# Rotation, modulation columns, masks and staged rows moved in a one-core trunk step

## The chip, the core and the metric

The kernel runs on one core of a Trainium2 chip. The metric is the device time of one launch in microseconds. TensorE is called PE (PEld are its weight loads), VectorE DVE, ScalarE ACT, GpSimd POOL, and SyncE SP; SP and POOL issue the DMAs.

## The reference

One layer of a hybrid trunk over 640 tokens (512 latent, 128 context) of width 1024: a gated feed-forward half-step, a token mixer, a second half-step, each behind a norm whose scale and shift (adaLN) come from a conditioning vector. Of the mixer, cut to what matters here:

```python
dq = rmsnorm(dq.reshape(B, T, DA_HEADS, 2, DA_HEAD_DIM), p['g_qn'][l])
dk = rmsnorm(dk.reshape(B, T, DA_HEADS, 2, DA_HEAD_DIM), p['g_kn'][l])
q_att = rope_2d(dq); keys = jnp.concatenate([rope_2d(dk), k_ctx], axis=1)
...
s = jnp.einsum('bqhcd,bkhcd->bhcqk', qi, kf) * scale
pr = jax.nn.softmax(s, axis=-1)
w = pr[:, :, 0] - lam * pr[:, :, 1]          # two softmaxes to a head
att = rmsnorm(einsum('bhqk,bkhv->bqhv', w, vf), g_sub)
...
# mLSTM, 4 heads, two directions, chunks of 128 tokens, state C carried on
dmat = jnp.exp(log_d - m_t[..., None])       # masked to the causal triangle
s = jnp.einsum('bhtd,bhsd->bhts', qc, kc) * dmat
num = einsum('bhts,bhsv->bhtv', s, vc) + inter * einsum('bhtd,bhdv->bhtv', qc, C)
...
y = sigmoid(gm) * (hm @ w_br_m) + sigmoid(gd) * (att @ w_br_d)
out = y @ w_out
```

The modulation is `silu(c) @ w_ada + b_ada`, 9 vectors of 1024 for each of two conditioning vectors. The outputs are the new tokens, the new keys and values of the context, and its final mLSTM states.

## The kernel before

Everything is float32, computed on PE as three products of split parts (a value is split into a high part and the remainder, and high x high, high x low and low x high are summed). ACT makes the high part of a weight (`wH`), DVE the low part (`wL`), from a raw row that SP loads.

The order of work on PE is the program's order (`mm` and `tr` keep it). The order of instructions on ACT, DVE, and the DMA queues is chosen by the scheduler when the kernel is built; each engine then works its list in order. `tc.issue_after(x)` puts the instructions of a block behind `x` on `x`'s engine.

*Attention, 8 heads* (profile from about 520 to 1075 us). Queries, keys and values are projected for pairs of heads. `qk_norm_rope` norms the projected rows and rotates them: the swapped copy `sw` on ACT, then on DVE `sw` times `B`, the rows times `A`, their sum, and the context tokens' gain. `Head.queries` and `Head.keys` turn the rows on PE into `ps_qkT`, ACT and DVE split them into `qT`, `kH` and `kL`, and POOL copies the halves of the keys to the other partitions. For each of five blocks of 128 queries: `scores` (PE into `sc`, then the softmax on DVE and ACT: `mx`, `nm`, two exponentials, `rc`, `r`, and `p`, kept as `at_p[qi]`), `turn` of the block before (PE into `ps_wT`), and `values` of it (PE into `ps_o`, DVE into `ao`, kept as `at_out`). Block 4 holds context tokens only and is short. After the last block comes the turn of the next head's queries and keys; if the next head is of a new pair, its keys must have been made (`made`).

Between these, `Fill` puts product units of other projections from a queue, so that PE has work while a softmax runs: `slot` runs at least one unit, and more where the pacing (`pace`, time per slot) says so. The units' results are evacuated into two staged rows (`stage`) and stored by SP: `o_evac` (DVE and ACT), `gate_evac` and `v_evac` (ACT). Two units stand ahead of head 0's first scores. The rows of the mLSTM gates are worked out in steps (`gate_rows`) beside head 0.

*Modulation columns.* `Columns.tile` loads a block of the turned modulation weights (512 KB, `raw_a`) and reduces it on DVE against the two conditioning vectors, two instructions of 128x1024 (`junk`). In attention eight tiles are placed in head 2 through one buffer, two after the values of each block from block 0 to block 3:

```python
            if qi > 0:
                H.values(qi - 1)
                if hd == 2:
                    columns.tile(H.at_out)
                    columns.tile(H.at_p[qi])
```

*mLSTM, 4 heads* (about 1075 to 1230 us). `Memory.load` brings values and the row of stabilisers, spread over the partitions, into `P`, and DVE adds the masks behind the last preparation of the head before. `prep` turns the keys, forms `ps_st`, takes the exponentials of `P` on ACT (`exps`) and multiplies on DVE. `cell` runs ten steps (five chunks, two directions): products with `P` and with the state `C`, and the update of `C` on DVE. A list `later` puts parts of the next and the last head behind the cells: preparations of the next head behind cells 3 to 7. `m.gate` loads `so` and takes its logarithm and exponential on ACT. Staged units of the gate projections run between the cells (`gate_evac` with the pool `mp`).

Of the kernel before, what the change touches and what calls it, by code (L numbers as in the profile page):

```python
# [31 lines left out]
def tile_trunk(ctx: ExitStack, tc: tile.TileContext, a: dict):  # L32
# [1137 lines left out]
    def qk_norm_rope(raw, tab, pr):  # L1170
        A, B, g = tab
        if pr:
            sq = ap.tile([128, 5, 256], F32, tag="pk", name="sq", bufs=2)
        else:
            sq = ap.tile([128, 5, 256], F32, tag="qT", name="sq")
        act(sq, raw, AF.Square)
        ss = ap.tile([128, 20], F32, tag="ss", name="ss", bufs=2)
        vec.tensor_reduce(out=ss, in_=sq.rearrange("p t (g d) -> p (t g) d", d=64), axis=AX.X, op=ALU.add)
        rs = rstd_of(ap, ss, 1.0 / 64, [128, 20], "qk")
        r3 = raw.rearrange("p t (g d) -> p (t g) d", d=64)  # L1180
        tt(vec, r3, r3, rs[:, :, None].to_broadcast([128, 20, 64]), ALU.mult)
        sw = ap.tile([128, 4, 256], F32, tag="pk", name="sw", bufs=2)
        act(
            sw.rearrange("p t (b s j) -> p (t b) s j", s=2, j=16),
            raw[:, 0:4, :].rearrange("p t (b s j) -> p (t b) s j", s=2, j=16)[:, :, ::-1, :],
            AF.Copy,
        )
        s4 = sw.rearrange("p t (g d) -> p t g d", d=64)
        q4 = raw[:, 0:4, :].rearrange("p t (g d) -> p t g d", d=64)
        tt(vec, s4, s4, B[:, :, None, :].to_broadcast([128, 4, 4, 64]), ALU.mult)  # L1190
        tt(vec, q4, q4, A[:, :, None, :].to_broadcast([128, 4, 4, 64]), ALU.mult)
        tt(vec, raw[:, 0:4, :], raw[:, 0:4, :], sw, ALU.add)
        p3 = raw[:, 4, :].rearrange("p (g d) -> p g d", d=64)
        tt(vec, p3, p3, g[:, None, :].to_broadcast([128, 4, 64]), ALU.mult)

    q_tok, k_tok, v_tok = {}, {}, {}
    made = set()

    def project_q(pr):
        def make():  # L1200
            q_tok[pr] = t = ap.tile([128, 5, 256], F32, tag="qtok", name="q_tok")

            def evac(p, i):
                act(t[:, i, :], p, AF.Copy)
                if i == 4:
                    qk_norm_rope(t, tabs[0], pr)

            return evac

        return a["w_dq"][pr], make  # L1210

    def project_k(pr):
        def make():
            k_tok[pr] = t = ap.tile([128, 5, 256], F32, tag="ktok", name="k_tok")

            def evac(p, i):
                act(t[:, i, :], p, AF.Copy)
                if i == 4:
                    qk_norm_rope(t, tabs[1], pr)
                    made.add(pr)  # L1220
                    nc.sync.dma_start(out=a["new_k"][:, pr * 256 : (pr + 1) * 256], in_=t[:, 4, :])

            return evac

        return a["w_dk"][pr], make
# [195 lines left out]
    def o_evac(h):  # L1421

        def f(p, mt, hf):
            t = ap.tile([128, HALF], F32, tag="stage", name="stage", bufs=2)
            ts(t, p, -43.0, ALU.max)
            act(t, t, AF.Exp, scale=-1.0)
            nc.sync.dma_start(out=o_dram[:, 2 * h + mt, half(hf)], in_=t)
        return f

    def gate_evac(pool, dst, g):  # L1430
        def f(p, mt, hf):
            t = pool.tile([128, HALF], F32, tag="stage", name="stage", bufs=2)
            act(t, p, AF.Copy)  # L1433
            nc.sync.dma_start(out=dst[:, 2 * g + mt, half(hf)], in_=t)
        return f

# [21 lines left out]
    for _ in range(3):  # L1458
        fill.one()
    heads[0].keys()  # L1460
    for _ in range(2):
        fill.one()
    heads[0].scores(0)

# [21 lines left out]

    def v_evac(h):
        def f(p, i):
            t = ap.tile([128, HALF], F32, tag="stage", name="stage", bufs=2)
            act(t[:, 0:256], p, AF.Copy)  # L1490
            nc.sync.dma_start(out=v_dram[h][:, i, :], in_=t[:, 0:256])
        return f
# [3 lines left out]
    for hd in range(8):  # L1496
        H = heads[hd]
        pr, odd = divmod(hd, 2)
        if not odd:
            fill.granule(a["w_mq"][pr], feat_units(psum, q_evac(pr)))  # L1500
            fill.granule(a["w_mk"][pr], feat_units(psum, k_evac(pr)))
            if pr:
                fill.granule(a["w_mv"][pr], tok_units(psum, v_evac(pr)))
            us = 2 * 13.2 + 13.0
            if hd == 0:
                us += 6 * 3.3
            if pr < 3:
                qk = project_q(pr + 1), project_k(pr + 1)
                fill.granule(qk[0][0], lambda f=qk[0][1]: tok_units(psum, f()), lambda hd=hd: turned > hd)
                fill.granule(qk[1][0], lambda f=qk[1][1]: tok_units(psum, f()), lambda hd=hd: turned > hd)  # L1510
                us += 26.0
            if not pr:
                fill.granule(a["w_mv"][pr], tok_units(psum, v_evac(pr)))
            if pr:
                fill.granule(a["w_mo"][pr], feat_units(psum, o_evac(pr)))
                us += 13.2
            if pr == 3:
                fill.granule(a["w_gd"][0], feat_units(psum, gate_evac(ap, gd_dram, 0)))
                fill.granule(a["w_gm"][1], feat_units(psum, gate_evac(ap, gm_dram, 1)))
                us += 16.0  # L1520
            fill.pace(us, 22)
        for qi in range(5):
            if hd or qi:
                H.scores(qi)
            if hd == 0 and qi < 4:
                with tc.issue_after(H.at_act.ins), tc.issue_after(H.at_p[qi - 1].ins if qi else H.at_vec.ins):
                    next(gates)
            if (hd, qi) == (1, 0):
                place_columns()
            if qi > 0:  # L1530
                H.turn(qi - 1)
            if hd == 1 and qi in (2, 3):
                gate_cols()
            fill.slot()
            if late is not None:
                late()
                late = None
            if hd == 1 and qi in (1, 2):
                gate_load(qi - 1)
            if qi > 0:  # L1540
                H.values(qi - 1)
                if hd == 2:
                    columns.tile(H.at_out)
                    columns.tile(H.at_p[qi])
            if qi < 4:
                fill.slot()
        H.turn(4)
        if hd < 7:
            N = heads[hd + 1]
            while N.pr not in made:  # L1550
                fill.one()
            if odd:
                fill.slot()
                H.values(4)
                src, evac = project_v(pr + 1)
                units = fill.begin(src, tok_units(psum, evac()))
                units[0]()
                N.queries()
                N.keys()
                turned = hd + 1  # L1560
                H.finish_norm()
                for u in units[1:]:
                    u()
            else:
                N.queries()
                N.keys()
                turned = hd + 1
                fill.slot()
                H.values(4)
                H.finish_norm()  # L1570
                fill.slot()
                fill.slot(2)
            late = H.finish
        else:
            fill.slot()
            H.values(4)
            H.finish_norm()
            fill.one()
            fill.one()
            fill.drain()  # L1580
            H.finish()
# [28 lines left out]
    class Memory:  # L1610
# [2 lines left out]
        def __init__(self, h):  # L1613
            self.h, self.cells = h, []

        def load(self, behind=None):
            h = self.h
            queue = nc.sync if h else nc.gpsimd
            self.va = mp.tile([128, 5, 258], F32, tag="va", name="va", bufs=2)
# [4 lines left out]
            for d in range(2):  # L1624
                queue.dma_start(
                    out=self.P[:, :, d, :], in_=nm_dram[32 * d + h].partition_broadcast(128).rearrange("p (c t) -> p c t", c=5)
                )
                with ExitStack() as st:
                    if behind is not None:
                        st.enter_context(tc.issue_after(behind.ins))  # L1630
                    tt(vec, self.P[:, :, d, :], self.P[:, :, d, :], mask[:, d, None, :].to_broadcast([128, 5, 128]), ALU.add)
            self.ktok = mp.tile([128, 5, 256], F32, tag="ktok", name="mktok", bufs=2)
            self.hs = mp.tile([128, 5, 256], F32, tag="hs", name="hs", bufs=2)

        def load_c(self):
            self.C = [mp.tile([128, 2, 258], F32, tag=f"C{d}", name="C", bufs=2) for d in range(2)]
# [7 lines left out]
        def prep(self, i):  # L1644
# [13 lines left out]
            for dt in range(2):  # L1658
                mm(p, k[:, dt, tok], q[:, dt, tok], start=dt == 0, stop=dt == 1)
            if h:  # L1660
                self.exps(i)
            self.at_prep = tt(vec, self.P[:, i], p[:, None, :].to_broadcast([128, 2, 128]), self.P[:, i], ALU.mult)

        def cell(self, i, d, accumulate, inter, update):
# [101 lines left out]
    mem = [Memory(h) for h in range(4)]  # L1766
    mem[0].load()
    mem[0].load_c()
    for i in range(5):
        mem[0].exps(i)  # L1770
    fill.one()
    fill.one()
    for i in range(5):
# [2 lines left out]
    for h in range(4):  # L1776
        m = mem[h]
        later = [[] for _ in range(10)]
        if h < 3:
            mem[h + 1].load(mem[h].at_prep)  # L1780
            for i in range(5):
                later[3 + i].append(lambda i=i: mem[h + 1].prep(i))
        if h > 0:
# [334 lines left out]
```

## Time and profile before

| | |
|---|---|
| median of 3 runs | 1856.08 us (1852.09 to 1860.09) |
| the profiled execution | 1852.26 us |
| its span, mean granted TensorE clock | 1850.4 us, 0.992 |
| PE busy in the span | 1791.7 us (97%) |
| DVE, ACT busy | 1291.0 us (70%), 829.7 us (45%) |

In the rows below, a timeline row has the start and the duration in us, the engine, the line of the kernel, the operation, out<-in with shapes, the count, and in brackets the idle time of the engine before it and what ended it. A row of stages has the stretch and its length, then busy times with counts of PE, PEld, DVE, ACT and POOL, the granted clock, the DMA share and GB/s. A row of waits has total, times and longest. A helper's instructions carry the helper's line: L52 `mm`, L55 `tr`, L39 `tt`, L42 `stt`, L46 and L48 `ts`.

### The profile page before, as it was taken

What the parts mean: (1) busy time and instruction counts of PE and PEld (TensorE: products, weight loads), DVE (VectorE), ACT (ScalarE), POOL (GpSimd) and SP (SyncE); (2) the same over time, 40 slices, a digit from 0 to 9 for tenths busy, and PEclk for the clock granted to TensorE, in tenths of its full rate; (3) what the DMA queues carried; (4) which work ended last, traced back from release to release, by engine and by line L of the source; (5) the groups of instructions that cost most, each with busy time, mean ns of one, the idle gap of its engine ahead of it and who ended that gap; (6) DMA issues with size and microseconds to landing.
All of it is one profiled execution on the core that took longest, in us unless ns stands there. A gap on an engine that the chain in (4) does not pass through costs nothing.

```text
span 1850.4 us, 30491 instructions
## 1 busy us (share of the span) xinstructions
PE 1791.7 (97%) x12498; PEld 1757.3 (95%) x12498; DVE 1291.0 (70%) x2188; ACT 829.7 (45%) x1439; POOL 51.6 (3%) x93
## 2 busy tenths in 40 slices
PE   6999999999999999999999999999999899999989
PEld 4999999999999998999999988899999899999989
DVE  6888885575776657765655557677767778886576
ACT  6654454112644543444443455573336455553232
POOL 0000001110000000000000000000000000000000
PEclk9999999999999999999999999999999999999989
DMA  8344448963324234232232254676652445557952
GB/s 332 130 161 171 155 150 325 328 209 120 119 88 151 73 122 139 74 119 75 83 101 91 97 168 130 208 250 213 211 182 75 154 149 169 189 172 277 342 205 85
DMA packets 127244, 304.98 MB, mean 165 GB/s; under 512 B 9985, under 2 KB 89217, under 8 KB 114433
## 3 DMA queue, kind: packets, MB, share of 16 engines
q1 hardware_dynamic: 116242, 257.09, 40.3%
q0 software_dynamic: 10864, 45.95, 7.2%
q8 instruction: 98, 1.61, 0.3%
q14 instruction: 40, 0.33, 0.1%
HBM read 234.20 MB, written 63.63 MB: 161 GB/s over the span
## 4 chain that ended last, share of the span: by engine, by line
PE 53%; DVE 3%; DMA 2%; ACT 1%; issue 1%; SPq 0%; DVEq 0%; ACTq 0%
PE ps_f L52 23%; PE ps_p L52 19%; PE ps_t L52 5%; PE ps_n L52 2%; PE sc L52 2%; PE ps_o L52 1%; PE ps_u L52 1%; DMA P<-nm_dram 1%; DMA raw_a<-in_w_ada_c 1%; PE ps_wT L55 1%; DVE wL L39 0%; ACT wH L122 0%; DVE k_tok L39 0%; DMA raw<-in_w_gm 0%; PE ps_st L52 0%
## 5 line engine op out<-in xcount | busy, mean ns | idle before, releaser
L52 PE MATMUL ps_f<-S,ww 128*128 128x320 f32 x1992 | 320.5, 311 | 5.5 <-ACT ww L286 3.8
L52 PEld LDWEIGHTS ps_f<-S,ww 128*128 128x128 f32 x1992 | 301.0, 189 | 6.1 <-ACT ww L286 4.1
L52 PE MATMUL ps_p<-hH,wH 128*128 128x320 f32 x864 | 274.1, 317 | 2.8 <-ACT stage L1433 1.6
L52 PE MATMUL ps_p<-hH,wL 128*128 128x320 f32 x864 | 267.6, 310 | 0.0
L52 PE MATMUL ps_p<-hL,wH 128*128 128x320 f32 x864 | 267.5, 310 | 0.0
L52 PE MATMUL ps_f<-hm,ww 128*128 128x320 f32 x1248 | 200.9, 314 | 7.6 <-ACT ww L286 4.1
L52 PEld LDWEIGHTS ps_f<-hm,ww 128*128 128x128 f32 x1248 | 190.3, 192 | 8.7 <-ACT ww L286 4.4
L52 PE MATMUL ps_t<-wH,hH 128*128 128x256 f32 x640 | 184.6, 288 | 4.3 <-ACT stage L1490 2.7
L52 PE MATMUL ps_t<-wH,hL 128*128 128x256 f32 x640 | 181.2, 283 | 1.1 <-DVE hL L39 1.1
L52 PE MATMUL ps_t<-wL,hH 128*128 128x256 f32 x640 | 180.9, 283 | 0.0
L52 PEld LDWEIGHTS ps_p<-hH,wH 128*128 128x128 f32 x864 | 163.1, 189 | 3.9 <-ACT stage L1433 1.9
L39 DVE TENSOR_TENSOR ww<-raw,ww 128x2048 fp32r<-128x2048 f32 (+1 forms) x62 | 138.7, 2237 | 39.9 <-ACT ww L286 26.2
L52 PEld LDWEIGHTS ps_p<-hL,wH 128*128 128x128 f32 x864 | 163.1, 189 | 0.5
L52 PEld LDWEIGHTS ps_p<-hH,wL 128*128 128x128 f32 x864 | 162.8, 188 | 0.0
L52 PE MATMUL ps_f<-hm,wB 128*128 128x320 f32 x1008 | 161.5, 309 | 0.0
L52 PEld LDWEIGHTS ps_f<-hm,wB 128*128 128x128 f32 x1008 | 151.3, 188 | 0.0
L39 DVE TENSOR_TENSOR wL<-raw,wH 128x2048 fp32r<-128x2048 f32 x49 | 112.1, 2288 | 43.7 <-ACT wH L122 43.6
L122 ACT ACTIVATE wH<-raw 128x2048 fp32r<-128x2048 f32 x49 | 93.6, 1911 | 81.7 <-PE ps_p L52 77.0
L52 PEld LDWEIGHTS ps_t<-wH,hH 128*128 128x128 f32 x640 | 122.5, 191 | 5.3 <-ACT stage L1490 2.9
L286 ACT ACTIVATE ww<-raw 128x2048 fp32r<-128x2048 f32 x48 | 91.7, 1911 | 75.0 <-DVE raw L39 63.7
L39 DVE TENSOR_TENSOR raw<-raw 128x1024 f32<-128x1024 f32 x144 | 124.2, 862 | 1.4
L52 PEld LDWEIGHTS ps_t<-wH,hL 128*128 128x128 f32 x640 | 122.5, 191 | 1.5 <-DVE hL L39 1.5
(295 smaller groups left out, 3179.9 us busy)
## 6 DMA issues: line engine op xcount, KB each, us to landing
g_dram<-g SPq DMA_DIRECT2D x44, 640.0 KB, 4.7
raw_a<-in_w_ada_c SPq DMA_DIRECT2D x32, 512.0 KB, 3.9
raw<-in_w1b SPq DMA_DIRECT2D x11, 1024.0 KB, 4.8
raw<-in_w3b SPq DMA_DIRECT2D x11, 1024.0 KB, 6.9
raw<-in_w1a SPq DMA_DIRECT2D x10, 1024.0 KB, 4.8
raw<-in_w3a SPq DMA_DIRECT2D x10, 1024.0 KB, 4.9
hm<-g_dram POOLq DMA_DIRECT2D x8, 1280.0 KB, 10.2
raw_a<-in_w_ada_k SPq DMA_DIRECT2D x8, 1024.0 KB, 11.3
```

The lines of the kernel that those rows point to most:

```text
L39: return eng.tensor_tensor(out=out, in0=in0, in1=in1, op=op)
L52: tc.keep_in_program_order(nc.tensor.matmul(*args, **kw))
L55: tc.keep_in_program_order(nc.tensor.transpose(*args, **kw))
L122: act(h, raw, AF.Copy)
L286: act(t[0], flat, AF.Copy)
```

## The change

The rotation of the keys becomes a generator of two steps. The first, up to the copy `sw`, comes where the whole came; the second is kept in `rotating` and issued, for pairs 1 to 3, behind the last softmax (`at_p[4]`) of the head that runs, and with it the store of the new keys. In attention there are three staged rows; four units instead of two stand ahead of head 0's scores. Of head 2's eight column tiles, one goes ahead of block 0, one behind its softmax, two after the values of blocks 0 and 1, none after block 2, one behind the last softmax and one after the last values. In the mLSTM stage the masks of the next head go behind cell 1, its exponentials behind the current cell's scaling on ACT, and the first staged row's evacuation behind head 0's exponentials.

```diff
             AF.Copy,
         )
+        yield
...
         tt(vec, p3, p3, g[:, None, :].to_broadcast([128, 4, 64]), ALU.mult)
+        yield
+
+    rotating = []
+
+    def rotated(behind=None):
+        while rotating:
+            with ExitStack() as st:
+                if behind is not None:
+                    st.enter_context(tc.issue_after(behind.ins))
+                rotating.pop(0)()
...
                 if i == 4:
-                    qk_norm_rope(t, tabs[1], pr)
-                    made.add(pr)
-                    nc.sync.dma_start(out=a["new_k"][:, pr * 256 : (pr + 1) * 256], in_=t[:, 4, :])
+                    steps = qk_norm_rope(t, tabs[1], pr)
+                    next(steps)
+
+                    def rest():
+                        next(steps)
+                        made.add(pr)
+                        nc.sync.dma_start(out=a["new_k"][:, pr * 256 : (pr + 1) * 256], in_=t[:, 4, :])
+
+                    rotating.append(rest)
+                    if not pr:
+                        rotated()
...
-            t = ap.tile([128, HALF], F32, tag="stage", name="stage", bufs=2)
+            t = ap.tile([128, HALF], F32, tag="stage", name="stage", bufs=3)
...
+    stage_behind = []
     def gate_evac(pool, dst, g):
         def f(p, mt, hf):
-            t = pool.tile([128, HALF], F32, tag="stage", name="stage", bufs=2)
-            act(t, p, AF.Copy)
+            t = pool.tile([128, HALF], F32, tag="stage", name="stage", bufs=2 + (pool is ap))
+            with ExitStack() as st:
+                for ins in stage_behind:
+                    st.enter_context(tc.issue_after(ins.ins))
+                act(t, p, AF.Copy)
+            stage_behind.clear()
...
-    for _ in range(2):
+    for _ in range(4):
         fill.one()
     heads[0].scores(0)
...
             if hd == 0:
-                us += 6 * 3.3
+                us += 4 * 3.3
...
+        if hd == 2:
+            columns.tile(H.at_vec)
         for qi in range(5):
...
             fill.slot()
+            if (hd, qi) == (2, 0):
+                columns.tile(H.at_p[0])
...
                 H.values(qi - 1)
-                if hd == 2:
+                if hd == 2 and qi < 3:
                     columns.tile(H.at_out)
                     columns.tile(H.at_p[qi])
+                if (hd, qi) == (2, 4):
+                    columns.tile(H.at_p[4])
+            if qi == 4:
+                rotated(H.at_p[4])
...
             while N.pr not in made:
                 fill.one()
+                rotated(H.at_p[4])
...
                 H.values(4)
+                if hd == 2:
+                    columns.tile(H.at_out)
                 H.finish_norm()
...
-        def load(self, behind=None):
+        def load(self):
...
+        def masks(self, behind=None):
+            for d in range(2):
                 with ExitStack() as st:
...
             if h:
-                self.exps(i)
+                with tc.issue_after(mem[h - 1].at_act.ins):
+                    self.exps(i)
...
     mem[0].load_c()
+    mem[0].masks()
     for i in range(5):
         mem[0].exps(i)
+    stage_behind.append(mem[0].at_exp)
...
-            mem[h + 1].load(mem[h].at_prep)
+            mem[h + 1].load()
+            later[1].append(lambda: mem[h + 1].masks(mem[h].at_vec))
```

More of the change, by code (lines that the diff above doesn't have):

```diff
@@ L1205, in evac @@
                 if i == 4:
-                    qk_norm_rope(t, tabs[0], pr)
+                    for _ in qk_norm_rope(t, tabs[0], pr):
+                        pass
             return evac
@@ L1488, in f @@
         def f(p, i):
-            t = ap.tile([128, HALF], F32, tag="stage", name="stage", bufs=2)
+            t = ap.tile([128, HALF], F32, tag="stage", name="stage", bufs=3)
             act(t[:, 0:256], p, AF.Copy)
@@ L1627, in load @@
                 )
+            self.ktok = mp.tile([128, 5, 256], F32, tag="ktok", name="mktok", bufs=2)
+            self.hs = mp.tile([128, 5, 256], F32, tag="hs", name="hs", bufs=2)
+        def masks(self, behind=None):
+            for d in range(2):
                 with ExitStack() as st:
@@ L1631, in load @@
                     tt(vec, self.P[:, :, d, :], self.P[:, :, d, :], mask[:, d, None, :].to_broadcast([128, 5, 128]), ALU.add)
-            self.ktok = mp.tile([128, 5, 256], F32, tag="ktok", name="mktok", bufs=2)
-            self.hs = mp.tile([128, 5, 256], F32, tag="hs", name="hs", bufs=2)
         def load_c(self):
```

## Prediction

> **What bounds the kernel now.** I read the page first, then the table of stages, then the waits of TensorE between 520 and 1230 us, then the timelines around each wait. Of the page, the first lines:
>
> ```profile
> span 1850.4 us, 30491 instructions
> ...
> PE 1791.7 (97%) x12498; PEld 1757.3 (95%) x12498; DVE 1291.0 (70%) x2188; ACT 829.7 (45%) x1439; POOL 51.6 (3%) x93
> ```
>
> TensorE (PE) is busy for 1791.7 of 1850.4 us. The change leaves every product in place, so all that it can win is idle time of PE, 58.7 us in all, and time that PE loses at a lowered clock. The stages, with PE's busy time as the second number of a row:
>
> ```profile
> 520.00:1075.00 555.00, 536.92 (x4065) 527.77 (x4064) 340.58 (x578) 241.95 (x479) 20.48 (x37) 1.00 0.31 101
> 1075.00:1225.00 150.00, 144.86 (x859) 132.98 (x860) 107.80 (x319) 90.38 (x225) 0.55 (x1) 1.00 0.54 173
> ```
>
> Attention (520 to 1075) has 18.1 us of idle PE, the mLSTM stage (1075 to 1225) 5.1. The diff touches these two alone, so 23.2 us, plus clock, is the ceiling: 1.25%. Who ends these idle times (total, times, longest):
>
> ```profile
> PE ps_wT L55 <- DVE p L42: 7.1, 4, 2.3
> PE sc L52 <- DMA kL<-kL: 3.3, 2, 2.9
> PE ps_t L52 <- ACT stage L1490: 2.7, 1, 2.7
> PE ps_n L52 <- ACT stage L1433: 1.9, 1, 1.9
> PE ps_aT L55 <- DVE ao L39: 1.8, 1, 1.8
> PE ps_p L52 <- ACT stage L1433: 1.6, 1, 1.6
> PE ps_n L52 <- ACT num L1680: 1.2, 1, 1.2
> PE ps_t L52 <- DVE qT L39: 1.2, 2, 0.6
> PE ps_p L52 <- DVE C L42: 1.1, 1, 1.1
> PE ps_k L55 <- DVE P L39: 0.9, 1, 0.9
> PE ps_t L52 <- ACT v_tok L1233: 0.5, 1, 0.5
> ```
>
> No engine is short of throughput here; each wait is one late item in an in-order queue. Of the first row the smallest and the one in head 2 are:
>
> ```profile
> 727.61 0.33 PE L55 MATMUL ps_wT<-ident,p 128*128 128x128 f32 x1 [1.78 <-DVE p L42]
> ...
> 1002.33 0.33 PE L55 MATMUL ps_wT<-ident,p 128*128 128x128 f32 x1 [0.70 <-DVE p L42]
> ```
>
> so the other two, in heads 3 and 5, are (7.1 - 1.78 - 0.70) / 2 = 2.31 each.
>
> **The change part by part.**
>
> *Four products instead of two ahead of head 0's scores.* Head 0's scores wait 3.3 us for the copies of the split keys, the last of which POOL issues late; one product of this kind takes 3.52:
>
> ```profile
> 533.16 0.52 POOL L1280 DMA_DIRECT2D kL<-kL  x1 [0.25 <-DVE kL L39]
> ```
> ```profile
> 782.36 3.52 PE ps_p L52 x24
> ```
>
> Two more are 7.0 us, over twice the wait: gain 3.3. They are taken from head 0's later slots (the pacing gives up 2 x 3.3), where at least one product stays in each slot and PE shows no other idle time in heads 0 and 1 but the last row's 0.5. The gate rows start some 4 us later against PE; their columns are used a whole head later, so this costs nothing.
>
> *Modulation columns of head 2.* Eight column tiles of two reductions each stand on DVE. Today two follow the values of each of blocks 0 to 3, and DVE runs the last four late, in the tail:
>
> ```profile
> 724.57 1.21 DVE L712 CUSTOM_DVE_ANT_0 junk<-raw_a,csil 128x1024 bf16<-128x1024 f32 x1
> ...
> 727.20 0.35 DVE L42 SCALAR_TENSOR_TENSOR p<-p,r,p 128x128 f32<-128x128 f32 x1
> ...
> 730.48 1.22 DVE L712 CUSTOM_DVE_ANT_0 junk<-raw_a,csil 128x1024 bf16<-128x1024 f32 x1 [2.92 <-DMA raw_a<-in_w_ada_c]
> ...
> 740.47 1.23 DVE L712 CUSTOM_DVE_ANT_0 junk<-raw_a,csil 128x1024 bf16<-128x1024 f32 x1 [2.12 <-DMA raw_a<-in_w_ada_c]
> ```
>
> The first row stands ahead of the last softmax (second row): PE waits 1.78. The third has DVE blocked 2.92 on a load, with the splits of the next queries behind it, behind these ACT's copies, and behind these the evacuation that PE waits 2.7 for. The fourth holds up the norm that PE's 1.8 wait for ao stands on. After: one tile ahead of the first block, one behind its softmax, two after the values of each of blocks 0 and 1, one behind the last softmax, one after the last values. Still eight, the same loads through one buffer, so SP issues the same; but two lie where DVE has little to do, and four are out of the way of the last softmax. Gains: 1.8 (0 to 1.8), 2.2 of 2.7 (the tile behind the last softmax still puts 2.4 us of DVE ahead of the query splits, but with its load long landed, so I leave 0.5), and 1.8 (0 to 1.8). Below nothing if the second of the two tiles after a block blocks DVE on its load as in the third row: -2.9 at worst, once. I take 5.8 together.
>
> *End of the key rotation behind the last softmax (pairs 2 and 3, in heads 3 and 5).* Before, DVE and ACT, then PE:
>
> ```profile
> 793.85 0.42 DVE L39 TENSOR_TENSOR k_tok<-k_tok,g_kn 128x256 f32<-128x256 f32 x1
> ...
> 794.25 1.22 DVE L39 TENSOR_TENSOR sw<-sw,ropeBk 128x1024 f32<-128x1024 f32 x1
> ...
> 796.52 0.48 DVE L46 TENSOR_SCALAR stage<-ps_p 128x320 f32<-128x320 f32 x1
> 796.92 0.15 DVE L1310 RECIPROCAL rc<-sm 128x2 f32<-128x2 f32 x1
> 796.99 0.33 DVE L1338 TENSOR_SCALAR ao<-ps_o,rc 128x128 f32<-128x128 f32 x1
> 797.24 1.22 DVE L39 TENSOR_TENSOR k_tok<-k_tok,sw 128x1024 f32<-128x1024 f32 x1
> 798.37 0.21 DVE L42 SCALAR_TENSOR_TENSOR r<-sm,nlam,rc 128x1 f32<-128x1 f32 x1
> 798.62 0.35 DVE L42 SCALAR_TENSOR_TENSOR p<-p,r,p 128x128 f32<-128x128 f32 x1
> ```
> ```profile
> 794.98 0.20 ACT L1309 ACTIVATION_READ_ACCUMULATOR p<-sc,nm 128x1 f32 x1
> ```
> ```profile
> 806.35 0.71 PE L55 MATMUL ps_qkT<-ident,k_tok 128*128 128x128 f32 x5
> ```
>
> ACT has the exponentials at 795.2, but p starts at 798.6, since three rotation steps of 1.2 stand ahead of parts of the chain rc, r, p. p ends at 799.0, where PE's wait of 2.31 ends; so PE was ready at 796.7. With the rotation behind, p can end at about 795.2 + 0.2 + 0.2 + 0.4 = 796.0, and PE goes on at once: 2.31, twice. What is late next: the rotation, 3 x 1.22 + 0.42 = 4.1 plus 0.8 for the staged row (0.48) and the attention row (0.33) in between, ends near 801; the store of the new keys and PE's key transposes stand behind it. PE gets to those at 806.35 - 2.31 = 804.0, so 3 us of slack remain; if the cover (one product, the last values, the first product of the next values) were gone, the price would be up to 4.1 per head. Pair 1 turns its keys after the last softmax already, pair 0 before any: nothing there. The two waits of 0.6 for qT stay, since they hang on ACT's split after PE's own product. The trace also shows one of the two gaps followed by slow products:
>
> ```profile
> 799.36 3.39 PE ps_p L52 x23
> ...
> 934.48 4.93 PE ps_p L52 x23
> ```
>
> The same 23 matmuls took 1.5 us more after head 5's gap than after head 3's, where the clock held. Without the gap this goes too: 1.4 (0 to 1.5). Part: 6.0. The Trainium skill, "TensorE: Matmul & The Clock Gate", Part 1, has the clock fall only after an idle window of about 3.4 us; by that rule a gap of 2.31 costs no clock, the term is nothing, and the time 1.4 higher. The two rows differ between themselves, which agrees with the free-running window of the same part, but a shorter gap than it states was enough here, so I go by the rows.
>
> *Three staged rows in attention.* I find no row where a product waits for a free staged row. PE's 1.6 at the start of the mLSTM stage is an evacuation queued behind a weight split:
>
> ```profile
> 1072.54 1.91 ACT L122 ACTIVATE wH<-raw 128x2048 fp32r<-128x2048 f32 x1 [2.94 <-PE ps_p L52]
> ```
>
> A third buffer may let that evacuation go ahead of the split (0 to 1.6) or only reorder stores. I take 0, the nearest: nothing in the trace says what set this order.
>
> *Masks, exponentials and the first staged row of the mLSTM stage.*
>
> ```profile
> 1089.31 3.03 ACT L1642 ACTIVATE P<-P,cols 128x128 f32<-128x128 f32 x10 [1.66 <-DVE P L39]
> ...
> 1175.31 1.27 ACT L1716 ACTIVATE so<-so 128x1280 f32<-128x1280 f32 x1 [0.77 <-DMA so<-o_dram]
> ```
> ```profile
> 1170.54 0.83 DVE L39 TENSOR_TENSOR P<-P,mask 128x640 f32<-128x640 f32 x1 [1.18 <-DMA P<-nm_dram]
> ```
>
> The masks wait at the head of DVE's queue for rows that DMA spreads over the partitions, and the updates of C queue behind (PE 1.1); ten exponentials of the next head block ACT for 3.0 (PE 1.2); head 0's own exponentials come after two staged rows (PE 0.9 for P). Masks behind cell 1, exponentials two by two behind the current cell's scaling, head 0's ahead of the first staged row: 1.1 + 1.2 + 0.9 = 3.2 (-1 to 3.2). The first evacuation then comes up to 3 us later and needs only a free bank, which PE does not lack there. The 1.9 wait ends with a staged row behind ACT's work on so, which waits for its own load, not for masks: I take 0.5 (0 to 1.9).
>
> **Sum.** 3.3 + 5.8 + 6.0 + 0 + 3.2 + 0.5 = 18.8. The new orders on DVE and ACT will make waits that no row shows yet; I put in one of the size of the largest present ones, 3 (0 to 6). Net 15.8. The profiled execution took 1852.26 us (span 1850.4): 1836.5. The median of the runs, 1856.08, lies 3.8 above the profiled one, within a spread of 8.0, so I say 1838 for a median. About 0.5% (9.3 us) is what this kernel's runs can tell from no change.
>
> **Rivals.** *Waits that move on (1842 to 1849).* What DVE lost to column loads in the whole kernel, total and times:
>
> ```profile
>   DMA raw_a<-in_w_ada_c: 12.9, 8
> ```
>
> If the loads through one buffer still block it in head 2 and the last rotation meets the transposes, parts two and three give 3 to 4 instead of 11.8, and the sum less 3 is 7 to 8. For it: the loads take as long as before. Against it: PE has products in between. *The change does not do what it says (1850 to 1858).* The orders come out of the scheduler at build; if it puts others in the place of those moved, only head 0's 3.3 is sure. Against it: the ties are fixed. *Slower (1862 or more).* One mechanism: in the mLSTM stage each of 15 preparations now has its product with P at the head of DVE's queue until ACT has done the scaling and two exponentials; today these lie done in a block (ten in 3.03). At about 1.6 us per preparation (0.6 for two, 1 for the hand-over and scaling, an estimate) with PE uncovered it is 24 us against 15.1 won in attention; it decides (9.3 above the profiled time) from (15.1 + 9.3) / 15 = 1.63 each on, and 2 us each gives 1867. Against it: PE has staged products between cells, and there is one preparation to a cell.
>
> **How the numbers follow.** Forecast (1830 to 1842) 0.62; waits that move on 0.22; nothing 0.09; slower 0.07. Under 1846.8 lie the first and most of the second: faster 0.76, same 0.17, slower 0.07. All terms at their best are 3.3 + 6.3 + 6.1 + 1.6 + 3.2 + 1.9 = 22.4, so 1830; the range goes from 2 below that, for the runs' spread, to the end of the second case: 1828 to 1850.
>
> **What would show it.** Right: idle PE of attention falls from 18.1 to about 6 and of the mLSTM stage from 5.1 to about 2; no wait for kL, none over 1 us for p; the three rotation steps follow p in heads 3 and 5, and PE's transposes of keys do not wait; no mask waits for DMA. Wrong: new waits of PE on k_tok, on P or on column loads, or a staged row that holds a bank at 1080.

## The result and the profile after

The changed kernel took 1830.94 us (median; 1828.53 to 1833.23) against 1856.08 us (1852.09 to 1860.09): a ratio of 0.9863, 95% interval 0.9843 to 0.9883. The forecast was 1838 us, range 1828 to 1850. By the medians the gain is 25.1 us, by the two profiled executions (1852.26 and 1830.94) 21.3; what follows accounts for the second. The profiled execution of the changed kernel has a span of 1829.2 us, 21.2 us less than before. First lines of its page:

```profile
span 1829.2 us, 30479 instructions
...
PE 1788.6 (98%) x12498; PEld 1757.0 (96%) x12498; DVE 1293.0 (71%) x2188; ACT 830.3 (45%) x1439; POOL 51.6 (3%) x93
```

PE's idle time fell from 58.7 us to 1829.2 - 1788.6 = 40.6 us, that is by 18.1, and its busy time by 3.1 with the same 12498 matmuls. The table of the two stages, after (PE busy is the second number):

```profile
520.00:1075.00 555.00, 551.21 (x4179) 542.51 (x4178) 351.08 (x599) 252.18 (x506) 21.03 (x38) 1.00 0.34 108
1075.00:1225.00 150.00, 148.83 (x893) 138.44 (x891) 114.22 (x338) 95.49 (x229) 0.00 (x0) 1.00 0.58 189
```

Of 23.2 us of idle PE in the two windows, 3.8 and 1.2 are left. PE's waits between 520 and 1230 us, after (total, times, longest); this is the whole list:

```profile
PE ps_t L52 <- DVE qT L39: 1.7, 3, 0.6
PE ps_n L52 <- ACT stage L1458: 1.2, 1, 1.2
PE ps_o L52 <- DVE wT L1347: 0.9, 1, 0.9
PE ps_wT L55 <- DVE p L42: 0.7, 1, 0.7
PE ps_t L52 <- ACT v_tok L1253: 0.5, 1, 0.5
```

Against the list of before: 3.3 for kL, 6.4 of 7.1 for p, 2.7 for the staged row L1490, 1.8 for ao, 1.6 for the staged row at the start of the mLSTM stage, 1.2 for num, 1.1 for C, 0.9 for P and 0.7 of 1.9 behind `so` went, 19.7 in all. New are 0.9 for wT and a third wait of 0.6 for qT. Net 18.2, against the 18.1 counted above.

Of the 3.1 us of busy time about half is clock in the two stages. The two product rows behind the softmax gaps of heads 3 and 5, from the chain after, are both short now (3.39 and 4.93 before), which is 1.5 us:

```profile
789.86 3.39 PE ps_p L52 x23
...
922.45 3.39 PE ps_p L52 x23
```

A span also holds clock changes outside the two stages. Most of those can be cut off by measuring between two landmarks of PE: the first product of the stage ahead of attention's scores, and the one long wait near the end, which every kernel here has. One lowered clock that no edit touches stays between them, at 1457.1 us before and 1437.6 us after. Before, then after:

```profile
472.35 0.28 PE L52 MATMUL ps_t<-wH,hH 128*128 128x256 f32 x1
...
1766.30 0.90 PE L52 MATMUL ps_f<-hm,ww 128*128 128x320 f32 x2 [4.13 <-ACT ww L286]
...
1768.62 7.89 PE L52 MATMUL ps_f<-hm,ww 128*128 128x320 f32 x34 [1.43 <-DVE ww L39]
```
```profile
473.95 0.28 PE L52 MATMUL ps_t<-wH,hH 128*128 128x256 f32 x1
...
1746.38 0.90 PE L52 MATMUL ps_f<-hm,ww 128*128 128x320 f32 x2 [4.13 <-ACT ww L286]
...
1748.70 6.58 PE L52 MATMUL ps_f<-hm,ww 128*128 128x320 f32 x34 [1.43 <-DVE ww L39]
```

Before 1766.30 - 472.35 = 1293.95 us, after 1272.43: 21.5 us gained. The last rows of the two fences show why a span alone misleads by a microsecond: 34 matmuls behind the same two waits took 7.89 and 6.58 us, and the changed kernel came 1.6 us later to the first landmark, though nothing is changed ahead of it. An unchanged copy of the changed kernel, run with the last experiments, has 1271.24 between the landmarks, so 1.2 us is what these two executions differ by; 1271.8, the mean of the two, is the reference below.

### The profile page after: what moved, and what is told of

It reads as the page before. It is cut to its first block, busy times and chain, and to the rows that moved or that the text cites. A ratio compares the mean times of both kernels' runs of the same rounds, so it can differ in the third digit from the quotient of the medians.

```text
span 1829.2 us, 30479 instructions
## 1 busy us (share of the span) xinstructions
PE 1788.6 (98%) x12498; PEld 1757.0 (96%) x12498; DVE 1293.0 (71%) x2188; ACT 830.3 (45%) x1439; POOL 51.6 (3%) x93
## 4 chain that ended last, share of the span: by engine, by line
PE 88%; DVE 5%; DMA 4%; ACT 2%; issue 1%; SPq 0%; DVEq 0%; ACTq 0%
PE ps_f L52 44%; PE ps_p L52 22%; PE ps_t L52 11%; PE sc L52 2%; PE ps_o L52 2%; PE ps_n L52 2%; DMA ada<-csil_dram 2%; PE ps_u L52 1%; PE ps_wT L55 1%; DVE junk L712 1%; DVE wL L39 1%; DMA raw_a<-in_w_ada_c 1%; DMA raw_a<-in_w_ada_k 1%; DMA x<-in_x 1%; DMA zT_dram<-so 0%
## 5 line engine op out<-in xcount | busy, mean ns | idle before, releaser
L52 PEld LDWEIGHTS ps_t<-wL,hH 128*128 128x128 f32 x640 | 122.6, 192 | 0.2
```

Source lines behind the costliest of these rows:

```text
L52: tc.keep_in_program_order(nc.tensor.matmul(*args, **kw))
```

## The experiments

Each is the changed kernel with one edit, unless it says otherwise. All landmarks in one table (us; the difference is against 1271.8). The last column counts the times that the clock granted to PE fell to half between 520 and 1230 us, each for 3.41 us, as the traces record it; behind the gap of head 5 before, one such time cost 4.93 - 3.39 = 1.5 us (more in the last section).

| kernel | first landmark | last landmark | between | difference | clock fell |
|---|---|---|---|---|---|
| before | 472.35 | 1766.30 | 1293.95 | +22.1 | 1 |
| changed | 473.95 | 1746.38 | 1272.43 | | 0 |
| changed, second copy | 474.14 | 1745.38 | 1271.24 | | 0 |
| two products | 474.33 | 1747.66 | 1273.33 | +1.5 | 0 |
| three products | 471.94 | 1746.05 | 1274.11 | +2.3 | 0 |
| columns as before | 472.57 | 1748.95 | 1276.38 | +4.5 | 1 |
| rotation at once | 472.76 | 1753.21 | 1280.45 | +8.6 | 2 |
| long rotation | 472.65 | 1745.94 | 1273.29 | +1.5 | 0 |
| before, three staged rows | 470.72 | 1766.43 | 1295.71 | +23.9 | 4 |
| two staged rows | 473.93 | 1744.54 | 1270.61 | -1.2 | 0 |
| mLSTM as before | 474.61 | 1750.71 | 1276.10 | +4.3 | 0 |
| masks as before | 474.49 | 1748.08 | 1273.59 | +1.8 | 0 |
| exponentials free | 474.82 | 1744.92 | 1270.10 | -1.7 | 0 |
| late gate | 472.23 | 1740.19 | 1267.96 | -3.9 | 0 |

### Products ahead of head 0's scores

Two instead of four, the pacing given back:

```diff
-    for _ in range(4):
+    for _ in range(2):
         fill.one()
     heads[0].scores(0)
...
-                us += 4 * 3.3
+                us += 6 * 3.3
```

> The changed kernel with two products instead of four ahead of head 0's scores (and the pacing as it was). Theory of the parts (each part takes away its own wait of PE): head 0's scores wait again for the copy of kL, 2.9 to 3.3 us in one or two waits; the 0.9 that the changed kernel waits for wT in head 0 goes; the span grows by 2.4 to 3.3 against 1829.2. Rival (waits move on, the parts are not separable): no wait for kL, or other waits change by over 1 us.

1833.65 us, span 1831.9. Its waits of PE have kL back, and the wait for wT is gone:

```profile
PE sc L52 <- DMA kL<-kL: 3.2, 2, 3.0
```

The wait behind `so` (1.2) is not in this kernel either. So the two products cover the copies of the split keys, and the 0.9 for wT is the price they pay: the gate rows of VectorE now fall into head 0's first turn. In the changed kernel, VectorE and then PE:

```profile
554.98 2.58 DVE L1116 TENSOR_TENSOR_SCAN rows<-rows,m 4x512 f32<-4x512 f32 x2
557.59 0.42 DVE L1347 COPY wT<-ps_wT 128x256 f32<-128x256 f32 x1
```
```profile
558.07 0.71 PE L52 MATMUL ps_o<-v_tok,wT 128*128 128x128 f32 x4 [0.88 <-DVE wT L1347]
```

Two scans, 2.58 us together, stand ahead of a copy of 0.42 that PE waits for. Would one product less avoid both? `range(3)`, with the pacing at `5 * 3.3`:

> The changed kernel with three products instead of four ahead of head 0's scores. Theory (3.52 of one product against 3.3 of wait): the wait for kL stays at 0, or at most 0.3, and the 0.9 for wT in head 0 goes, since the gate rows start earlier against PE: span 0.5 to 0.9 shorter. Rival: the wait for wT does not hang on this, or kL is later: same or up to 1 longer.

1831.75 us, span 1830.0. One product more than before is enough for kL, which shows no wait. But wT stayed, at 1.2, and a wait appeared that the changed kernel does not have, the one of before at the start of the mLSTM stage:

```profile
PE ps_p L52 <- ACT stage L1458: 1.6, 1, 1.6
PE ps_o L52 <- DVE wT L1347: 1.2, 1, 1.2
```

That half of the expectation fell: the same two scans still stand ahead of the copy (548.11 to 550.69 us, the copy at 552.40), now with a maximum of 1.76 us in between. The new wait matters for the question of the third staged row, next.

### The third staged row

`bufs=2` in attention again (`two_rows`), and on the other side the kernel of before with three rows alone (`rows_alone`):

> The changed kernel with two staged rows in attention instead of three. Every engine's instructions stand in the same order as with three, so only the waits for a row to be stored differ. Theory (the third row is worth the 1.6 at the start of the mLSTM stage): PE waits 1.6 for a staged row there again, span 1.5 to 3 longer. Rival (that wait went with the others, and the third row does nothing): within 0.5 of 1829.2.

1830.0 us, span 1828.2 (1.0 less than with three), the same list of waits but for 0.6 instead of 1.2 behind `so`, and all engines have their instructions in the same order as with three.

> The kernel before with three staged rows in attention and nothing else; the instructions keep their order on every engine. Theory (the third row is worth the 1.6): the wait at the start of the mLSTM stage goes, span 1.5 shorter than 1850.4, the other waits as before; if the third row also has a share in the 2.7 for a staged row in head 2, that wait falls too. Rival: all waits stay.

1851.09 us, span 1849.2 (1850.4 before), and 1.8 us more than before between the landmarks. The wait in question still stands:

```profile
PE ps_p L52 <- ACT stage L1433: 1.6, 1, 1.6
```

Other waits are smaller than before, which the expectation leaves open for one of them: 1.9 instead of 2.7 for the staged row L1490, 0.6 instead of 1.8 for ao, 0.9 instead of 1.9 behind `so`; the list adds up to 20.3 instead of 23.3. The trace explains the first two without the third row. SP issues the load that stands in front of L1490 at the same time (725.79 us, before 725.82), and VectorE could use it after 3.9 us instead of 4.7. Behind this wait the clock fell, so that PE came later to ao and waited less there. In all the clock fell three times more than before; at 1.53 each that is 4.6 us, against 3.0 less of waits: 1.6 of the 1.8.

So no part of the gain is shown to come from the third row: without it the changed kernel is as fast, and alone it does not take away the 1.6. The 1.6 us were won by something else. In the traces, the first weight load of the mLSTM stage carries a wait on ScalarE before, with three rows alone and with three products, and none with four or two. Its product starts at 1074.83 us before, behind the evacuation (1074.36, 0.42 long), and at 1059.37 in the changed kernel, ahead of it (1060.77). The evacuation stands behind the same weight split in both, so what differs is whether the product needs what that evacuation frees. That this is a PSUM bank is argued, not shown, and the number of products ahead does not settle it alone: the kernel of before has two and waits, the changed kernel with two does not.

### Modulation columns of head 2

The tiles of head 2 back in their places of before, two behind each block:

```diff
-        if hd == 2:
-            columns.tile(H.at_vec)
...
-            if (hd, qi) == (2, 0):
-                columns.tile(H.at_p[0])
...
-                if hd == 2 and qi < 3:
+                if hd == 2:
                     columns.tile(H.at_out)
                     columns.tile(H.at_p[qi])
-                if (hd, qi) == (2, 4):
-                    columns.tile(H.at_p[4])
...
-                if hd == 2:
-                    columns.tile(H.at_out)
                 H.finish_norm()
```

> The changed kernel with head 2's column tiles where they were. Theory of the parts: the three waits in the tail of head 2 come back, 1.8 for p, 2.7 for a staged row and 1.8 for ao, together 6.2, and the 0.6 for qT there goes; the span grows by 5 to 6.5. If the third staged row alone had taken the wait for the staged row, only 3.5 come back.

1834.81 us, span 1833.0. The waits came back in the same places, but not in full: 1.4 for p, 2.5 for the staged row and 0.3 for ao, 4.2 of the expected 6.2, and the span grew by 3.8, less than the 5 to 6.5 expected. VectorE and then PE:

```profile
727.55 1.23 DVE L712 CUSTOM_DVE_ANT_0 junk<-raw_a,csil 128x1024 bf16<-128x1024 f32 x1 [2.68 <-DMA raw_a<-in_w_ada_c]
```
```profile
724.93 0.33 PE L55 MATMUL ps_wT<-ident,p 128*128 128x128 f32 x1 [1.44 <-DVE p L42]
...
731.66 0.39 PE L52 MATMUL ps_t<-wH,hH 128*128 128x256 f32 x1 [2.45 <-ACT stage L1516]
```

VectorE stands 2.68 us for a load with the query splits behind it (their first starts at 728.82), and PE waits 2.45. Right behind this wait, at 732.8 us, the clock fell, which it did not at this place before; PE then came later to ao, which explains the small wait there. With 0.5 less for qT, as expected, and 0.8 less behind `so`, the waits are 2.9 more than in the changed kernel; with 1.5 for the clock that is 4.4 of the 4.5 between the landmarks. With the tiles where the change puts them, VectorE waits 3.3 us for such loads between 640 and 760 us, in 3 places, where it waited 9.5 in 5 before; none of the three is in the tail behind the last softmax.

### End of the key rotation

Rotation at once for all pairs:

```diff
-                    if not pr:
-                        rotated()
+                    rotated()
```

> The changed kernel with the whole rotation of the keys issued where the last key product ends, not behind the last softmax. Theory of the parts: PE waits for p in heads 3 and 5 by 2.3 each, 4.6 in all, and each of these gaps may or may not be followed by a microsecond or two of slow products (the clock fell after one of the two before): span 4.6 to 7.7 longer, PE's busy time up by 0 to 3. Rival (the gaps came from the whole order in these heads, staged rows included): one wait or none, under 2.5.

1839.26 us, span 1837.4: the largest of the four undos, 8.2 in the span, a little over the expected range. Its wait row, then the products behind the two gaps, from its chain:

```profile
PE ps_wT L55 <- DVE p L42: 5.3, 3, 2.3
```
```profile
791.67 4.92 PE ps_p L52 x23
...
928.32 4.92 PE ps_p L52 x23
```

5.3 - 0.7 is twice 2.3. Both gaps now cost clock too: 4.92 against 3.39 for the same 23 products, 1.53 each. 4.6 + 3.1 = 7.7 of the 8.6 between the landmarks.

How much slack does the rotation have where it is now? Four more products of 128x1024 into the scratch `sw`, which nobody reads afterwards, in pairs 2 and 3:

```diff
+        if pr > 1 and tab is tabs[1]:
+            for _ in range(4):
+                tt(vec, sw, sw, raw[:, 0:4, :], ALU.mult)
```

> The changed kernel with four more DVE products (128x1024, 1.22 each, into a scratch row that nobody reads) in the end of the rotation of pairs 2 and 3, ahead of the context tokens' gain: 4.9 us more between the last softmax and the key transposes. Theory (about 3.6 us of slack there hide the rotation): PE waits 1 to 1.5 for the keys, or up to 4 where the splits of the next values queue behind too, in each of heads 3 and 5; span 2 to 8 longer. Rival (other work covers it, the slack is larger): no new wait.

1832.03 us, span 1829.9; PE has no wait for k_tok, but five of 0.5 for v_tok instead of one, and one of 0.6 for qT instead of three. VectorE's rows say that this tested less than was meant:

```profile
790.73 1.21 DVE L39 TENSOR_TENSOR k_tok<-k_tok,sw 128x1024 f32<-128x1024 f32 x1
...
801.07 1.21 DVE L39 TENSOR_TENSOR sw<-sw,k_tok 128x1024 f32<-128x1024 f32 x1
```

The added products came behind the last step of the keys, so this step was not later than in the changed kernel. What is shown is that VectorE has room there for 4.9 us more work per head at about 1 us of cost in all (+0.7 in span, +1.5 between the landmarks, noise 1.2); the slack of the rotation itself must be read from the trace (below).

### The mLSTM stage

Masks, exponentials and first staged row all as before:

```diff
-    stage_behind.append(mem[0].at_exp)
...
-                with tc.issue_after(mem[h - 1].at_act.ins):
-                    self.exps(i)
+                self.exps(i)
...
-            later[1].append(lambda: mem[h + 1].masks(mem[h].at_vec))
+            mem[h + 1].masks(mem[h].at_prep)
```

> The changed kernel with masks, exponentials and the first staged row of the mLSTM stage as they were. Theory of the parts: DVE waits for DMA ahead of the masks again (about 8 us over five or six) and PE for P, num and C, 3.2 in all, and the wait behind so goes from 1.2 back to 1.9: span 3 to 4 longer. Rival: the waits of this stage hang on the time at which it starts, and under 1.5 comes back.

1836.61 us, span 1834.8, 5.6 more and so over the expected 3 to 4; 4.3 between the landmarks. Its new waits of PE:

```profile
PE ps_n L52 <- DVE C L42: 1.4, 1, 1.4
...
PE ps_k L55 <- DVE P L39: 0.9, 1, 0.9
PE ps_u L52 <- ACT wv L1724: 0.8, 1, 0.8
```

That is 3.1, less 0.5 because the wait behind `so` is 0.7 here: 2.6 of the 4.3, and the rest is in no wait of the stage. The wait for num (1.2 before) did not return, one for wv stands in its place. Then two of the three parts alone.

> The changed kernel, with the mask additions of heads 1 to 3 of the mLSTM stage issued with their loads again; its exponentials and its first staged row stay as changed. Theory A (the masks carry most of the mLSTM part): vector work that waits for a transfer stands ahead of state updates, so VectorE shows over 7 us of waits for P from nm_dram again, in 6 places, and TensorE waits 1.4 us for C (the wait that came back when all three parts were undone): span 1.4 to 2.3 us longer. Theory B (the masks only cost in company with the exponentials): the waits of VectorE for P are back but TensorE waits for no C, and the span moves by less than 0.7 us.

1833.71 us, span 1831.9, +1.8. VectorE's waits, and PE's largest:

```profile
DVE P L39 <- DMA P<-nm_dram: 10.7, 6, 4.0
```
```profile
PE ps_n L52 <- DVE C L42: 2.1, 1, 2.1
```

Theory A holds, with the span a little above its range: a mask that waits 4.0 us for its rows at the head of VectorE's queue holds up one update of C for 2.1 us. Less the 1.2 behind `so`, which is gone in this kernel, 0.9 is left, half of the +1.8.

> The changed kernel, with the exponentials of heads 1 to 3 of the mLSTM stage no longer tied behind the previous copy wv. Theory A: they stand ahead of wv again, and TensorE's waits for wv (0.8 us) and for P (0.9 us) are back: span 1.5 to 2 us longer. Theory B (they only stood in the way when the masks came late): no wait for wv of over 0.3 us, and the span moves by less than 0.7 us.

1830.66 us, span 1828.9, -1.7. Theory B: no wait for wv and none for P. The wait behind `so` is gone, and ScalarE's rows show why:

```profile
1154.70 1.27 ACT L1756 ACTIVATE so<-so 128x1280 f32<-128x1280 f32 x1 [0.80 <-DMA so<-o_dram]
...
1156.28 0.41 ACT L1458 ACTIVATE stage<-ps_p 128x320 f32<-128x320 f32 x1
...
1156.95 1.26 ACT L1757 ACTIVATE so<-so 128x1280 f32<-128x1280 f32 x1
```

The staged row got between the two passes over `so`. With the masks early enough, tying the exponentials wins nothing. The third part, the first staged row, was not undone by itself; PE's wait of 0.9 for P came back only where it was undone with the others.

### Two of the remaining waits taken away

The logarithm and exponential of `so` after the third cell of the next head, and the reduction `ass` behind the next head's last key split in heads 1, 3 and 5:

```diff
         def gate(self):
...
-            with tc.issue_after(self.at_act.ins):
-                act(self.so, self.so, AF.Ln, bias=1.0)
-                act(self.so, self.so, AF.Exp, scale=-1.0)
+            if h == 3:
+                self.sigmoid(self)
...
+        def sigmoid(self, m):
+            with tc.issue_after(m.at_act.ins):
+                act(self.so, self.so, AF.Ln, bias=1.0)
+                act(self.so, self.so, AF.Exp, scale=-1.0)
...
         if h > 0:
+            later[2].append(lambda: mem[h - 1].sigmoid(mem[h]))
...
-                H.finish_norm()
+                H.finish_norm(N.at_vec)
```

It ran beside the second copy of the changed kernel:

> The changed kernel once more, unchanged, beside the next one. All theories: 1829 to 1834 us, 0.984 to 0.988 of the time before.

> The changed kernel with two of the waits taken away that the change left: the logarithm and exponential of `so` of heads 0 to 2 are issued after the third cell of the following head instead of behind their load, and in heads 1, 3 and 5 the reduction `ass` goes behind the last split of the next head's keys instead of standing ahead of `qT`. Theory A (each wait is one of the order alone): the wait of 1.17 us behind `so` and two waits of 0.58 us for qT are gone, nothing takes their place, idle time of TensorE between 520 and 1225 us falls from 5.0 to 2.7 us, and the time is 2.3 us under the unchanged copy. Theory B (the waits move on): the reduction's 0.81 us delays kL or ao instead, the so of the next head comes too late for its product, and the time is within 1 us of the copy. Both are near what five rounds can tell apart, so the waits decide.

The copy took 1828.80 us, 0.9863 of before (0.9845 to 0.9881); late gate took 1826.58 us, 0.9856 (0.9839 to 0.9874). The medians are 2.2 us apart and the intervals overlap, so the gain in time is not shown; the waits are. The copy has the same list as the first one, with 1.3 instead of 1.2 behind `so`. PE's whole list in late gate:

```profile
PE ps_o L52 <- DVE wT L1347: 0.9, 1, 0.9
PE ps_t L52 <- DVE qT L39: 0.8, 2, 0.6
PE ps_wT L55 <- DVE p L42: 0.7, 1, 0.7
```

Idle PE in the two windows, late gate:

```profile
520.00:1075.00 555.00, 552.64 (x4181) 543.76 (x4180) 353.46 (x608) 253.43 (x511) 21.05 (x38) 1.00 0.34 109
1075.00:1225.00 150.00, 150.00 (x910) 140.48 (x909) 115.00 (x335) 95.12 (x224) 0.00 (x0) 1.00 0.59 197
```

2.4 us are left, of 5.0, all of it in attention; by the waits, theory A. The mLSTM stage has no idle PE at all, so any further idle PE lies in other stages.

## Why the prediction was right, and where it was off

*The bound.* PE's idle time and clock in two stages were called the ceiling, 23.2 us; 18.1 and 1.5 came from there. Right.

*Four products.* +3.3 predicted for kL; the wait went, and the 0.9 for wT came with it: 2.4. The sentence that the later gate rows cost nothing was the error: their columns are indeed used much later, but the scans themselves stand in VectorE's queue ahead of a copy that is needed at once.

*Columns.* +5.8 predicted, 1.8 + 2.7 + 1.8 = 6.3 gone and one wait of 0.6 for qT new: 5.7 by the waits, 4.5 by the undo. The undo brought back 4.2 of the three waits and 1.5 of clock, less what the waits for qT and behind `so` lost there. I left 0.5 of the 2.7 for the tile behind the last softmax, and the 0.6 appeared behind it; heads 3 and 5 have the same wait for qT without a tile, so that the tile makes it is not shown.

*Rotation.* +6.0 predicted (two gaps of 2.31 and 1.4 of clock); two gaps of 2.3 and 1.5 of clock measured. That the clock term fits is luck: the clock had fallen behind one of the two gaps in the one execution that I read, and it fell behind both in two other kernels with the same gaps, where the part is worth 7.7 (4.6 and 3.1). Slack of the keys: predicted some 3 us. In head 3, VectorE and then PE, after:

```profile
788.86 0.34 DVE L42 SCALAR_TENSOR_TENSOR p<-p,r,p 128x128 f32<-128x128 f32 x1
789.12 1.22 DVE L39 TENSOR_TENSOR sw<-sw,ropeBk 128x1024 f32<-128x1024 f32 x1
...
791.99 1.22 DVE L39 TENSOR_TENSOR k_tok<-k_tok,sw 128x1024 f32<-128x1024 f32 x1
```
```profile
796.86 0.71 PE L55 MATMUL ps_qkT<-ident,k_tok 128*128 128x128 f32 x5
```

The last step ends at 793.2 and PE comes at 796.86: 3.65. The order is the one predicted, p first.

*Third staged row.* 0 predicted, and no effect shown by either experiment. But the 1.6 that I named with it as its upper bound went all the same, by luck: no part of the change was aimed at it, and why it went is open (above). This is the first mis-sized term: a wait that I read as one of the queue's order also depends on whether the product needs that evacuation at all, and I had no row for that.

*mLSTM stage.* +3.2 predicted as three separate waits (C 1.1, num 1.2, P 0.9); all three went, and undoing the parts together brings 3.1 of waits back. The split was wrong: the masks are the part that matters (they bring back 2.1 for C by themselves; VectorE's wait for their rows is 8.6 us in 6 places before and 0.5 in one after), and the tie of the exponentials is worth nothing alone. Its rows, before and after, among what VectorE waits for in front of P:

```profile
  DMA P<-nm_dram: 8.6, 6
```
```profile
  DMA P<-nm_dram: 0.5, 1
```

*Behind `so`.* +0.5 (0 to 1.9) predicted, 0.7 less in the profiled execution. That the change did this is not shown: in eight traces with the mLSTM stage as changed the wait is anything from 0 to 1.6, and with three rows alone, where the stage is as before, it is 0.9 instead of 1.9. What is left after the change is as described, a staged row behind both passes over `so`, of which the first waits for its load; ScalarE, then PE, after:

```profile
1153.89 1.27 ACT L1757 ACTIVATE so<-so 128x1280 f32<-128x1280 f32 x1 [2.80 <-DMA so<-o_dram]
...
1156.63 0.41 ACT L1458 ACTIVATE stage<-ps_p 128x320 f32<-128x320 f32 x1
```
```profile
1157.09 1.14 PE L52 MATMUL ps_n<-C,mqT 128*128 128x258 f32 x4 [1.17 <-ACT stage L1458]
```

*New waits.* -3 (0 to 6) predicted, -1.5 measured. This is the second mis-sized term; I took the size of the largest present waits, and what moved on was of the size of the smallest.

*The sum.* 15.8 predicted, 21.3 measured between the profiled executions. Of the 5.5, the staged row at the start of the mLSTM stage is 1.6, the new waits 1.5 (0.9 and 0.6, which I had as 3), `so` and columns together 0.7 (0.2, and the 0.5 that I left of 2.7 and counted again as a new wait), the clock at the end of the program 1.3 less the 1.6 lost at its start, and 2.0 are not located, more than the 1.2 by which the two copies differ. The other 1.6 between 1838 and 1830.94 is how the forecast was placed: I added 1.5 because the profiled execution of before was faster than the median of its runs, and that of the changed kernel lies on its median. The result lies at the lower end of the range, 1 us above the sum of all terms at their best (1830). By the medians the gain, 25.1, is more than that best sum, 22.4; the 2.0 and this remainder are found in no row.

*The rivals.* Waits that move on: one of 0.9 and one of 0.6, not 8 us of them. No effect: excluded by the time. Of the undos, 4.5, 8.6 and 4.3 us are clear of the 1.2 between the copies; the 1.5 of two products rests on its wait of 3.2 for kL. The slower case, P's products held behind the exponentials: PE never waits for P after the change.

## What to carry to other kernels

Where the main engine is 97% busy, list its waits and find, for each, the instruction that stands ahead of the late one in an in-order queue; moving that behind the urgent one was worth the whole wait here, twice 2.3 us for the rotation, since the moved work had slack, which can be read beforehand from when its consumer comes. Work that waits for a transfer (the masks, the column tiles) is bad to have ahead, because it blocks the queue without using it: one tile held VectorE for 2.68 us, and PE waited 2.45. When something small is moved elsewhere, ask not only when its result is used but what is queued behind it, as the scans ahead of wT were.

## What the runs showed of the hardware

A gap of 2.31 us in PE's work was enough to lower the clock in five of the six such gaps profiled, behind the softmaxes of heads 3 and 5 in the kernel of before, in rotation at once and in the kernel of before with three rows: the 23 products took 4.92 or 4.93 us behind five of them, and 3.39 behind one. PE in the last of these kernels, in head 3:

```profile
798.51 0.33 PE L55 MATMUL ps_wT<-ident,p 128*128 128x128 f32 x1 [2.31 <-DVE p L42]
...
799.01 0.47 PE L52 MATMUL ps_p<-hH,wL 128*128 128x320 f32 x1
799.27 0.47 PE L52 MATMUL ps_p<-hH,wH 128*128 128x320 f32 x1
...
802.21 0.37 PE L52 MATMUL ps_p<-hH,wL 128*128 128x320 f32 x1
802.41 0.31 PE L52 MATMUL ps_p<-hH,wH 128*128 128x320 f32 x1
```

The products start 0.27 us apart from 799.01 to 802.21 and 0.15 apart from 802.41 on: some 3.2 us at little over half speed, which costs 1.5. The trace records a granted clock of 0.50 from 798.9 to 802.3 us, 3.41 us long. The Trainium skill, "TensorE: Matmul & The Clock Gate", Part 1, gives about 3.4 us of sustained work before the clock is back at full speed, which agrees with this stretch; the idle window of the same length that it states ahead of the drop does not agree with drops behind 2.31 us.

The length of the gap does not decide it. The granted clock is 1.00 or 0.50, and its changes in a trace lie whole multiples of 3.413 us apart, to 3 ns. If each of the 14 traces is cut along this grid into stretches of 3.413 us, from 60 us to the last product, 7180 of them run at full clock. In 49 of these PE idles for 1.86 us or more, and the next stretch ran at 0.50 each time; in all others PE idles for 1.82 us or less, and the next ran at 1.00. So in these traces the clock falls when PE has idled for a little over half of one stretch, and a gap that lies across two stretches can cost nothing. Some gaps, with the idle time of PE in the fullest stretch:

| kernel, gap of PE | gap, us | idle in one stretch, us | next clock |
|---|---|---|---|
| before, p in head 3 | 2.31 | 1.59 | 1.00 |
| before, p in head 5 | 2.31 | 2.31 | 0.50 |
| before, L1490 in head 2 | 2.69 | 1.56 | 1.00 |
| two products, kL | 3.01 | 1.71 | 1.00 |
| columns as before, L1516 in head 2 | 2.45 | 2.23 | 0.50 |
| before with three rows, L1490 in head 2 | 1.89 | 1.89 | 0.50 |

A gap of 2.31 us therefore costs 1.5 us beyond itself or nothing, and which it is can change when only something earlier has moved, since that moves the gap against the grid. The ends of matmuls are modelled in a profile, so the 1.82 and 1.86 are no sharper than that.

Executions of the same program differ by about 1 us (1.2 between the two copies), and behind equal waits the 34 products above took 7.89 or 6.58 us in places that no edit touched, so single edits of this size were read from waits and between landmarks, not from the time.
